# High weights against both halves of the activations: one product of 512 columns where there were two of 256

## The chip, the core and the metric

The kernel runs on one core of a Trainium2 chip. A core has a matrix engine (PE; the loading of its weights is listed as PEld), a vector engine (DVE), a scalar engine (ACT), a general engine (POOL) and a queue engine that issues the transfers (SP). Each works through its own list of instructions in order and waits on semaphores of the others. The metric is device time of one execution: 2247.73 us before the change, the median of three runs (2246.83 to 2248.64).

## The reference, cut to what matters

Two transformer blocks over 256 tokens of width 2048. The first (sparse attention, pooling, a mixture of 32 experts) is computed by instructions that the change leaves alone. The second has two layers:

```python
def even_layer(h, ...):                                   # layer 0
    z = h @ w_in                                          # 2048 x 4352
    lru_x, lru_gate, q, k, v, swa_gate = split_cols(z, EVEN_SPLITS)
    y_a = rg_lru(causal_depthwise_conv(lru_x, ...), ...) * silu(lru_gate)
    y_b = sliding_window_gqa_sinks(q, k, v, sinks) * silu(swa_gate)
    return concatenate([y_a, y_b]) @ w_out                # 2048 x 2048
def odd_layer(h, ...):                                    # layer 1
    z = h @ w_in                                          # 2048 x 6464
    c_q, c_kv, k_rope, mla_gate, dq, dk, dv, diff_gate = split_cols(z, ODD_SPLITS)
    ...
    return concatenate([y_c, y_d]) @ w_out
for layer in (0, 1):
    x = x + layer(rmsnorm(x, gain))
return rmsnorm(x, final_gain)
```

## The kernel before, in words

**Split products.** Every float32 matrix of the dense products is split into two halves of a shorter type (fp32r): a high half h (a cast on ACT, `ACT.copy(h, t)` in `prep`) and a low half l (a subtraction on DVE, `tt(l, t, f32(h), OP.subtract)` in `low`). A product is then three: high weights times high activations, high weights times low activations, low weights times high activations, all added up in the same place in PSUM.

**Chunks and steps.** `dense` computes a chunk of n output columns. In the form "T" the weights (128 rows x 128 columns) are PE's stationary operand, and the 256 tokens of the activations move through, so a group of 128 output columns (an m-tile) fills half a PSUM bank of 512 columns. In the form "tok" it is the other way round: the activations of 128 tokens are stationary and 512 weight columns move. `weight_steps` cuts a chunk into steps. For n = 512 a step holds 2 of the 16 row tiles k, for n = 256 it holds 4. A step of the form T at n = 512 is 2 x 4 x 3 = 24 products of 256 columns; a step of the form tok is 12 products of 512 columns. Each step has a raw weight tile (one of two 1 MB places, each of which serves two steps; SP loads it in pieces of 512 KB), a tile of halves (one of four places) and the products.

**Order.** The program writes out its order itself. In `run_steps` (ahead = 3, lag = 1), round i issues the load and cast of step i + 3, then the subtraction of step i + 2, then the products of step i, then one `bg.tick()`: one piece of the background tasks (recurrence, attention, norms) and one piece of the chain of evictions. In what follows a *round* is that. A chunk's evictions come one a round after its last step (`one_by_one`), and for the first chunk of a layer not before the norm of the tokens is ready. `scaled` multiplies an m-tile out of PSUM by that norm on DVE (`y<-acc,vr`, `dv<-acc,vr`, `z<-acc,vr`); `Join` combines a gate (its Tanh on ACT) with what it gates.

**Places.** PSUM has four banks "acc" for dense products, so two chunks of two banks; three banks "tps" for attention and transposes, one "ada". The next chunk but one takes a chunk's banks over.

**Attention.** `attend` works in rounds as well. For head i the scores are made (PE, L818, L1711), the masked scores and their extreme are taken (DVE, L749), the exponentials (ACT, L753; L756 for the sink), the division (DVE, L771); PE transposes P two rounds (L781, sliding window) later, the result is copied (PT, in turns by ACT and DVE), and the product with the values follows (L810, L812, L1744 to L1746). The stretches of the trace: recurrence 1490 to 1600 us, sliding window 1618 to 1690, layer 1 from about 1760, latent attention 1932 to 2005, differential attention 2044 to 2110, output projection and end from 2136.

Of the kernel before, what the change touches and what calls it, by code (L numbers as in the profile page):

```python
# [4 lines left out]
F32 = mybir.dt.float32  # L5
# [137 lines left out]
def fused_kernel(tc, a, out):  # L143
# [30 lines left out]
    with top:  # L174
# [261 lines left out]
        class Wide:  # L436


            def __init__(self, pool):
                self.pool, self.x, self.r, self.ready = pool, ({}, {}), {}, False  # L440
# [4 lines left out]
            def halves(self, j):  # L445
                r = []
                for i in (0, 1):
                    n = 2 * (j // 4) + i
                    if n not in self.r:
                        self.r[n] = self.pool.tile([128, 4, 2, S], F32R, name=f"a{n}")  # L450
                    r.append(self.r[n][:, j % 4])
                    for k in (0, 1):
                        self.x[i][2 * j + k] = r[i][:, k]
                return r
# [44 lines left out]
        def weight_steps(w, KT, c0, n, mm, done, load=None, order=None, apart=0):  # L499


            steps, late = [], []
            cell = {}
            order = order or [(k0, min(4, KT - k0)) for k0 in range(0, KT, 4)]
            b = 4 if n <= 256 else 2
            ks = [(k0, kn, k) for k0, kn in order for k in range(k0, k0 + kn, b)]
            for i, (k0, kn, k) in enumerate(ks):

                def prep(k0=k0, k=k, kn=kn):
                    if k == k0:  # L510
                        cell["raw", k0] = t = raw()
                        if load:
                            load(t, k0, kn)
                        else:
                            for k1 in range(0, kn, pieces[0]):
                                kk = min(kn - k1, pieces[0])
                                SP.dma_start(t[:, k1:k1 + kk, 0:n],
                                             w[(k0 + k1) * 128:(k0 + k1 + kk) * 128, c0:c0 + n]
                                             .rearrange("(k p) n -> p k n", p=128))
                    t = cell["raw", k0][:, k - k0:k - k0 + b, 0:n]  # L520
                    x = half_places.next()
                    if b == 4:
                        x = x.rearrange("p k (i n) -> p (k i) n", i=2)
                    h, l = x[:, 0:b, 0:n], x[:, b:2 * b, 0:n]
                    cell[k] = (h, l, t)
                    ACT.copy(h, t)  # L526

                def low(k=k):
                    h, l, t = cell[k]
                    tt(l, t, f32(h), OP.subtract)  # L530

                def step(k=k, i=i, ts=(0, 1)):
                    for j in range(b):
                        mm(k + j, cell[k][0][:, j], cell[k][1][:, j], i + j == 0, i + 1 == len(ks) and j + 1 == b, ts)
                    if i + 1 == len(ks):
                        done(ts)
                if i < len(ks) - apart:
                    steps.append(Dense(prep, step, low))
                else:
                    steps.append(Dense(prep, (lambda f=step: f(ts=(0,))), low))  # L540
                    late.append(Dense(lambda: None, (lambda f=step: f(ts=(1,)))))
            return steps + late

        def dense(w, KT, c0, n, acts, outs, load=None, order=None, apart=0):


            regs, bank, off = [], -1, 512
            for kind, arg, m, ev in outs:
                for t in ((0,) if kind == "T" else (0, 1)):
                    wd = S if kind == "T" else m  # L550
                    if off + wd > 512:
                        bank, off = bank + 1, 0
                    regs.append((kind, arg, m, ev, t, bank, off, wd))
                    off += wd
# [6 lines left out]
            def mm(k, h, l, first, last, ts):  # L561
# [3 lines left out]
                for r in regs:  # L565
                    kind, arg, m, _, t, b, o, wd = r
                    if t not in ts:
                        continue
                    if kind == "T":
# [11 lines left out]
            def out(r, x):  # L581
                return (r[3](x) if r[0] == "T" else r[3](r[4], x)) or ()
# [18 lines left out]
            return weight_steps(w, KT, c0, n, mm, done, load, order, apart)  # L601

# [850 lines left out]
        ytile = lambda i, c, dt=F32R: yt.tile([128, S], dt, name=f"y{i}_{c}")  # L1453

        class Join:
# [16 lines left out]
            def join(self, c, slot, src, gate, scale):  # L1472
# [6 lines left out]
                h, l = (ytile(i, self.first + c) for i in (0, 1))  # L1479
# [3 lines left out]
                self.yT[0][self.first + c], self.yT[1][self.first + c] = h, l  # L1483
# [9 lines left out]
        hT, yT = norm.hT, [{}, {}]  # L1493
# [11 lines left out]
        lo_slot = lambda first: lambda c: ytile(1, first + c, F32)  # L1505
# [89 lines left out]
        steps += dense_T(wi0, KD, 512, 512, hT, to_xr)  # L1595
        steps[7].then = lambda: bg.add(lru(0))
        steps[15].then = lambda: bg.add(lru(1))
        for c0 in (2048, 2560):
            steps += dense_T(wi0, KD, c0, 512, hT, lambda c, p: norm.scaled(q0[:, c - 16], p))
        steps += dense(wi0, KD, 3072, 256, hT, [("T", 0, 128, k_ev), ("T", 128, 128, lambda p: norm.scaled(vT0, p))])  # L1600
        steps[-1].then = lambda: bg.add(swa())
        for c0 in (1024, 1536):
            steps += dense_T(wi0, KD, c0, 512, hT, lambda c, p: join_a(c - 8, p, True))
        for c0 in (3328, 3840):
            steps += dense_T(wi0, KD, c0, 512, hT, lambda c, p: join_b(c - 26, p, True))
# [4 lines left out]
        x, y, *z = [dense_T(wo0, KD, n0, 512, yT, add_xT)  # L1610
                    for n0 in range(0, D, 512)]
# [17 lines left out]
        def odd():  # L1629
            hT, yT = norm1.hT, [{}, {}]  # L1630
# [25 lines left out]
            def scratch(i, c):  # L1656
                if (i, c) not in held:
                    held[i, c] = ytile(i, c, F32)
                return held[i, c]
# [116 lines left out]
            steps = dense_T(wi1, KD, 0, 512, hT, to_c) + dense_T(wi1, KD, 512, 512, hT, to_c)  # L1776
# [3 lines left out]
            for c0 in (2368, 2880):  # L1780
                steps += dense(wi1, KD, c0, 512, hT, [("T", m * 128, 128, (lambda p, h=(c0 - 2368) // 128 + m: norm1.scaled(dqT(h), p)))
                                                      for m in range(4)])
# [33 lines left out]
            for c0 in (3392, 3904):  # L1816
                steps += dense(wi1, KD, c0, 512, hT, [("T", m * 128, 128, (lambda p, h=(c0 - 3392) // 128 + m: norm1.scaled(dkT(h), p)))
                                                      for m in range(4)])
# [8 lines left out]
            for c0 in (1344, 1856):  # L1827
                steps += dense(wi1, KD, c0, 512, hT, [("T", m * 128, 128, (lambda p, c=(c0 - 1344) // 128 + m: join_c(c, p, True)))
                                                      for m in range(4)])
            for c0 in (5440, 5952):  # L1830
                steps += dense(wi1, KD, c0, 512, hT, [("T", m * 128, 128, (lambda p, c=(c0 - 5440) // 128 + m: join_d(c, p, True)))
                                                      for m in range(4)])
# [71 lines left out]
```

## Time and profile before

| | |
|---|---|
| time, median of three runs | 2247.73 us |
| time of the profiled execution | 2247.3 us |
| its span | 2245.5 us |
| PE busy over the span | 1900.1 us (85%) |
| DVE, ACT busy over the span | 989.5 us (44%), 629.7 us (28%) |
| the second block's dense stretch, 1476 to 2231 us | PE busy 754.95 of 755 us |

Busy time is an average over stages of different kinds: the first 1400 us wait for transfers of expert weights, the rest is PE's. A wait in brackets behind a row is the time that its engine sat idle before that instruction, and whom it waited for. The ends of PE's rows are modelled, so PE is read from start to start.

### The profile page before, as it was taken

What the parts mean: (1) busy time and instruction counts of PE and PEld (TensorE: products, weight loads), DVE (VectorE), ACT (ScalarE), POOL (GpSimd) and SP (SyncE); (2) the same over time, 40 slices, a digit from 0 to 9 for tenths busy, and PEclk for the clock granted to TensorE, in tenths of its full rate; (3) what the DMA queues carried; (4) which work ended last, traced back from release to release, by engine and by line L of the source; (5) the groups of instructions that cost most, each with busy time, mean ns of one, the idle gap of its engine ahead of it and who ended that gap; (6) DMA issues with size and microseconds to landing.
All of it is one profiled execution on the core that took longest, in us unless ns stands there. A gap on an engine that the chain in (4) does not pass through costs nothing.

```text
span 2245.5 us, 35044 instructions
## 1 busy us (share of the span) xinstructions
PE 1900.1 (85%) x14718; PEld 1369.9 (61%) x14718; DVE 989.5 (44%) x1866; ACT 629.7 (28%) x1072; POOL 73.3 (3%) x90
## 2 busy tenths in 40 slices
PE   5999999986768676666767575999999999999998
PEld 3666656662424242423333242699989999989986
DVE  2456736541212122121212120667886657556864
ACT  2333324311000000000000010355664444435543
POOL 2000100000000000000000000000000001200000
PEclk8999999998898788898989898999999999999999
DMA  9999898889999999999999999855536556444554
GB/s 336 382 359 338 318 379 297 307 345 410 389 420 421 421 420 421 421 421 421 421 421 420 421 413 422 310 177 169 181 124 187 177 171 179 150 150 151 169 188 149
DMA packets 198066, 694.94 MB, mean 309 GB/s; under 512 B 20455, under 2 KB 44553, under 8 KB 140433
## 3 DMA queue, kind: packets, MB, share of 16 engines
q1 hardware_dynamic: 194608, 682.03, 79.9%
q0 software_dynamic: 2000, 6.89, 1.0%
q10 hardware_dynamic: 1296, 3.74, 0.4%
q8 instruction: 117, 1.92, 0.3%
q14 instruction: 45, 0.36, 0.0%
HBM read 690.49 MB, written 2.11 MB: 308 GB/s over the span
## 4 chain that ended last, share of the span: by engine, by line
PE 42%; DMA 27%; DVE 2%; ACT 1%; issue 1%; SPq 0%; POOLq 0%; POOL 0%; ACTq 0%; DVEq 0%
PE acc L578 31%; DMA w<-in_w_dram 14%; DMA a<-in_w_dram 8%; PE acc L1151 4%; DMA wx<-in_w_dram 3%; DMA h<-in_w_dram 2%; PE acc L1186 2%; DVE Og L167 1%; PE acc L1216 1%; PE acc L1378 1%; PE tps L818 1%; PE tps L781 1%; PE tps L1711 0%; PE ada L810 0%; PE tps L1560 0%
## 5 line engine op out<-in xcount | busy, mean ns | idle before, releaser
L578 PE MATMUL acc<-h,h 128*128 128x512 f32 (+1 forms) x1152 | 277.4, 390 | 13.2 <-DVE h L167 5.2
L1186 PE MATMUL acc<-w,Xg 128*32 128x256 f32 x2176 | 213.1, 447 | 71.7 <-DMA w<-in_w_dram 71.2
L578 PEld LDWEIGHTS acc<-h,h 128*128 128x128 f32 x1152 | 203.4, 191 | 92.5 <-issue 23.6
L167 DVE TENSOR_TENSOR s<-s,acc 64x256 f32<-64x256 f32 (+1 forms) x34 | 14.9, 438 | 431.4 <-ACT s L1193 427.0
L1186 PEld LDWEIGHTS acc<-w,Xg 128*32 128x32 f32 x2176 | 92.5, 124 | 171.1 <-DMA w<-in_w_dram 103.0
L1193 ACT ACTIVATE s<-acc 64x256 f32<-64x256 f32 x32 | 12.1, 377 | 620.1 <-PE acc L1186 620.1
L167 DVE TENSOR_TENSOR Og<-acc,gt 32x512 f32<-32x512 f32 x124 | 85.2, 687 | 212.9 <-PE acc L1216 211.3
L1186 PE MATMUL acc<-a,Xg 128*32 128x256 f32 x1312 | 131.1, 455 | 52.9 <-DMA a<-in_w_dram 43.2
L167 DVE TENSOR_TENSOR h<-w,h 128x1024 fp32r<-128x1024 f32 (+2 forms) x106 | 124.3, 1176 | 67.6 <-ACT h L526 66.4
L526 ACT CAST h<-w 128x1024 fp32r<-128x1024 f32 (+2 forms) x106 | 105.7, 1002 | 108.5 <-PE acc L578 51.4
L1186 PEld LDWEIGHTS acc<-a,Xg 128*32 128x32 f32 x1312 | 56.3, 126 | 112.3 <-DMA a<-in_w_dram 60.8
L578 PE MATMUL acc<-a,w 128*128 128x256 f32 x948 | 122.1, 285 | 0.1
L578 PE MATMUL acc<-a,wx 128*128 128x256 f32 x948 | 121.8, 285 | 0.2 <-DVE wx L167 0.2
L1151 PE MATMUL acc<-Ps,x 128*128 128x128 f32 x448 | 99.4, 395 | 25.4 <-DVE Ps L1139 25.4
L578 PE MATMUL acc<-a,h 128*128 128x256 f32 (+1 forms) x924 | 118.9, 285 | 0.4 <-DVE h L167 0.4
L1151 PEld LDWEIGHTS acc<-Ps,x 128*128 128x128 f32 x448 | 98.3, 311 | 34.1 <-issue 34.1
L578 PEld LDWEIGHTS acc<-a,wx 128*128 128x128 f32 x948 | 116.4, 191 | 2.5 <-issue 2.0
L578 PEld LDWEIGHTS acc<-a,w 128*128 128x128 f32 x948 | 116.6, 191 | 1.8 <-issue 0.7
L578 PEld LDWEIGHTS acc<-a,h 128*128 128x128 f32 (+1 forms) x924 | 113.5, 191 | 2.1 <-issue 1.3
L578 PE MATMUL acc<-a,gt 128*128 128x256 f32 (+1 forms) x876 | 112.3, 284 | 0.0
L578 PEld LDWEIGHTS acc<-a,gt 128*128 128x128 f32 (+1 forms) x876 | 107.6, 191 | 1.8 <-issue 1.7
L1216 PE MATMUL acc<-w,aT 128*32 128x512 f32 x528 | 76.1, 675 | 34.0 <-DMA w<-in_w_dram 27.9
(496 smaller groups left out, 2816.7 us busy)
## 6 DMA issues: line engine op xcount, KB each, us to landing
w<-in_w_dram SPq DMA_DIRECT2D x205, 1024.0 KB, 19.8
a<-in_w_dram SPq DMA_DIRECT2D x116, 1024.0 KB, 19.8
w<-in_l_w_in_dram SPq DMA_DIRECT2D x160, 512.0 KB, 4.6
w<-in_w_ada_dram SPq DMA_DIRECT2D x42, 1024.0 KB, 7.5
w<-in_l_w_out_dram SPq DMA_DIRECT2D x64, 512.0 KB, 4.7
wx<-in_w_dram SPq DMA_DIRECT2D x30, 1024.0 KB, 19.8
h<-in_w_dram SPq DMA_DIRECT2D x29, 1024.0 KB, 19.8
w<-in_w_ada_dram SPq DMA_DIRECT2D x30, 512.0 KB, 10.1
```

The lines of the kernel that those rows point to most:

```text
L167: (e or DVE).tensor_tensor(out=o, in0=x, in1=y, op=op)
L526: ACT.copy(h, t)
L578: PE.matmul(out_of(r), lt, rt, start=first and i == 0 and o == 0, stop=last and i == 2, skip_group_check=True)
L781: PE.transpose(p[:, b * 128:(b + 1) * 128], P[h][:, b * 128:(b + 1) * 128], ident)
L818: PE.matmul(p[:, r], q[:, t * 128:(t + 1) * 128], k[:, 0:128 * (t + 1)], start=True, stop=True)
L1151: PE.matmul(b[:, (k - k0) * 128:(k - k0 + 1) * 128], x1[:, t, k:D:16], flat(Ps)[:, t], start=t == 0, stop=t == 1)
L1186: PE.matmul(p1[32 * j:32 * j + 32, 0:256], Xg[:, k, 32 * el:32 * el + 32], w[:, k % 4, (j % 2) * 256:(j % 2) * 256 + 256], start=k == 0, s ...
L1193: ACT.activation(s[0:64], p1[0:64, 0:256], AF.Silu)
L1216: PE.matmul(p2[32 * j:32 * j + 32, :], aT[:, kk % 2, (kk // 2) * 32:(kk // 2) * 32 + 32], down[kk][:, j * 512:(j + 1) * 512], start=kk == ...
L1378: PE.matmul(p, PWT[:, t * 128:(t + 1) * 128], Og[:, n:n + 512], start=True, stop=True)
```

## The change

A new form `dense_2T` replaces `dense_T` for 19 of the 512-column pieces of the second block: all but the first of layer 0's input projection, the last two of its output projection, and all T pieces of layer 1's input projection of width 1024 (latents, queries, keys and gates). It cuts each into two chunks of 256 columns. The two halves of the activations now lie side by side in one tile, and a product with the high weights moves both, 512 columns, into a whole bank; the product with the low weights moves the high half alone, 256 columns, into the bank's first half. At eviction ACT copies the bank's second half to SBUF, DVE adds the first half to it, and the old eviction goes on from the sum.

```diff
+            narrow = n == 256 and KT == KD and not order
+            kt = 8 if narrow else 4
...
+                            part = pieces[0] * kt // 4
+                            for k1 in range(0, kn, part):
+                                kk = min(kn - k1, part)
...
+            both = 2 if apart is None else 1
+            apart = apart or 0
...
-                    wd = S if kind == "T" else m
+                    wd = (S * both if kind == "T" else m)
...
+                    if kind == "T" and both == 2:
+                        PE.matmul(out_of(r).rearrange("p (i s) -> p i s", i=2), h[:, arg:arg + m], acts[2][k],
+                                  start=first, stop=False, skip_group_check=True)
+                        PE.matmul(out_of(r)[:, 0:S], l[:, arg:arg + m], acts[0][k], start=False, stop=last,
+                                  skip_group_check=True)
...
             def out(r, x):
+                if both == 2:
+                    side[0] ^= 1
+                    y = summed[0:x.shape[0], side[0]]
+                    ACT.copy(y, x[:, S:2 * S])
+                    tt(y, y, x[:, 0:S], OP.add)
+                    x = y
...
+        def dense_2T(w, KT, c0, n, acts, ev):
+            r = []
+            for c in range(c0, c0 + n, 256):
+                r += dense(w, KT, c, 256, acts, [("T", m, 128, (lambda p, c=(c + m) // 128: ev(c, p))) for m in (0, 128)], apart=None)
+            return r
...
+        summed = pp.tile([128, 2, S], F32, name="sel")
```

A raw tile of 1 MB now holds 8 row tiles of 256 columns in place of 4 of 512, in rows of 1 KB in place of 2 KB, still two steps' worth and still in pieces of 512 KB.

The first place where the order changes is on PE, early in layer 0. There the first chunk (banks acc_8653 and acc_8654) is still of 512 columns, and the norm becomes ready in round 10. PE at the end of step 11 and the start of step 12 in the kernel before (a0 to a3: activations; wx_8972, h_9009: the halves of the weights of the steps 11 and 12):

```order
L578 MATMUL acc_8976<-a1_8567,wx_8972 128x256
L578 MATMUL acc_8976<-a0_8566,wx_8972 128x256
L578 MATMUL acc_8975<-a2_8703,h_9009 128x256 [waits Activation_49]
L578 MATMUL acc_8975<-a3_8704,h_9009 128x256
L578 MATMUL acc_8975<-a2_8703,h_9009 128x256 x2
L578 MATMUL acc_8975<-a3_8704,h_9009 128x256
L578 MATMUL acc_8975<-a2_8703,h_9009 128x256
```

PE at the end of step 11 and the start of step 12 in the changed kernel (here a0 and a3 are tiles that hold both halves of the activations):

```order
L576 MATMUL acc_8977<-a3_8718,wx_8973 128x512
L578 MATMUL acc_8977<-a3_8718,wx_8973 128x256
L576 MATMUL acc_9075<-a0_8566,h_9002 128x512 [waits DVE_49,Activation_49]
L578 MATMUL acc_9075<-a0_8566,h_9002 128x256
L576 MATMUL acc_9076<-a0_8566,h_9002 128x512 [waits DVE_49]
```

Before, step 12 goes on in the banks of the second chunk. Now step 12 opens a third chunk, which takes over the two banks of the first, each after a wait for DVE. The count that the second of these waits for stands at the fourth of the evictions shown next.

DVE at the same place in the changed kernel, rounds 10 to 13 (dv<-acc: evictions of the first chunk; 128x1024 rows: the low halves of the steps 13 to 15); the kernel before has the same rows here, under other buffer numbers:

```order
L1339 TENSOR_SCALAR PT<-K,rs 128x128 x2
L167 TENSOR_TENSOR dv<-acc,vr 128x256
L167 TENSOR_TENSOR gt_9021<-w_8999,gt_9021 128x1024
L167 TENSOR_TENSOR dv<-acc,vr 128x256
L167 TENSOR_TENSOR w_9052<-w_9049,w_9052 128x1024
L167 TENSOR_TENSOR dv<-acc,vr 128x256
L167 TENSOR_TENSOR wx<-w_9049,wx 128x1024
L167 TENSOR_TENSOR dv<-acc,vr 128x256
```

Nothing moved in this list: what is new is that PE's step 12 waits for its last row, which stands behind the low half of step 15.

The second place is a round of the sliding window attention in which an m-tile of a gate is evicted. DVE before (P, st: scores and sums of a head; y_10931: the gate's m-tile):

```order
L749 ISA P_10916,st_10923<-tps_10917,masks_8736,sink_3575 128x256
L749 ISA st_10923 128x1
L167 TENSOR_TENSOR y_10931<-acc_10455,vr_9069 128x256
L167 TENSOR_TENSOR gt2_10869<-w0_10816,gt2_10869 128x1024
L167 TENSOR_TENSOR y1_8_10908<-y_10905,y0_8_10907 128x256
L164 SCALAR_TENSOR_TENSOR y1_11_10930<-y1_11_10930,y_10931 128x256
```

DVE in the changed kernel:

```order
L777 ISA P_10509,st_10516<-tps_10510,masks_8737,sink_3575 128x256
L777 ISA st_10516 128x1
L167 TENSOR_TENSOR sel_8730<-sel_8730,acc_10307 128x256
L167 TENSOR_TENSOR y_10526<-sel_8730,vr_9046 128x256
L167 TENSOR_TENSOR wx_10469<-w1_10423,wx_10469 128x1024
L167 TENSOR_TENSOR y8_10501<-y_10499,y8_10501 128x256
L164 SCALAR_TENSOR_TENSOR y11_10525<-y11_10525,y_10526 128x256
```

ACT in the same round of the changed kernel:

```order
L781 ACTIVATE P_10509,st_10516<-P_10509,st_10516 128x128
L781 ACTIVATE P_10509,st_10516<-P_10509,st_10516 128x256
L784 ACTIVATE st_10516<-sink_3575,st_10516 128x1 x2
L597 COPY sel_8730<-acc_10307 128x256
L1519 ACTIVATE y11_10525<-y_10526 128x256
L530 CAST h_10532<-w0_10529 128x1024
```

DVE's eviction now begins with a sum that reads what ACT's COPY wrote, and that COPY stands behind the four exponentials of the head in the same round.

## Rows read from the trace of the kernel before

**Rows 1.** Windows: us, busy PE, PEld, DVE, ACT, POOL, PEclk, DMA share, GB/s.

```profile
1476.00:2231.00 755.00, 754.95 (x5693) 712.08 (x5692) 506.39 (x919) 382.62 (x645) 35.76 (x33) 1.00 0.53 165
1618.00:1690.00 72.00, 72.00 (x602) 64.90 (x601) 59.04 (x184) 47.56 (x137) 0.00 (x0) 1.00 0.39 127
1938.00:1985.00 47.00, 47.00 (x337) 41.73 (x336) 21.84 (x55) 16.61 (x35) 0.00 (x0) 1.00 0.37 117
2044.00:2110.00 66.00, 66.00 (x554) 62.42 (x554) 57.54 (x177) 39.51 (x105) 0.00 (x0) 1.00 0.41 129
```

**Rows 2.** Chain of waits from 1690 to 1940 us: start, us, what.

```profile
1774.09 74.54 PE acc L578 x624
```

**Rows 3.** Timeline of PE at a tok chunk's end: start, us, engine, line, what.

```profile
2032.55 2.88 PE L578 MATMUL acc<-h,a 128*128 128x512 f32 x12
2035.27 3.04 PE L578 MATMUL acc<-a,gt 128*128 128x256 f32 x24
...
2041.02 3.04 PE L578 MATMUL acc<-a,wx 128*128 128x256 f32 x24
```

**Rows 4.** Timeline of PE in the two latent up-projections.

```profile
1875.19 2.99 PE L578 MATMUL acc<-z,gt 128*128 128x256 f32 x24
1878.02 2.99 PE L578 MATMUL acc<-z,w 128*128 128x256 f32 x24
...
1898.52 0.88 PE L578 MATMUL acc<-gt,dv 128*128 128x256 f32 x6
1899.24 0.88 PE L578 MATMUL acc<-dv,gt 128*128 128x256 f32 x6
```

**Rows 5.** Timeline of PE, steps 11 to 13 of layer 0.

```profile
1476.20 3.11 PE L578 MATMUL acc<-a,wx 128*128 128x256 f32 x24
1479.15 3.04 PE L578 MATMUL acc<-a,h 128*128 128x256 f32 x24
1482.03 3.04 PE L578 MATMUL acc<-a,gt 128*128 128x256 f32 x24
```

**Rows 6.** Timeline of DVE in the same stretch.

```profile
1480.43 1.23 DVE L167 TENSOR_TENSOR wx<-w,wx 128x1024 fp32r<-128x1024 f32 x1 [0.18 <-ACT wx L526]
1481.57 0.42 DVE L167 TENSOR_TENSOR dv<-acc,vr 128x256 f32<-128x256 f32 x1
```

**Rows 7.** Timeline of all engines in the sliding window attention.

```profile
1618.92 0.37 ACT L153 COPY P<-tps 128x256 f32<-128x256 f32 x1 [2.01 <-PE tps L1525]
...
1638.17 0.35 DVE L749 CUSTOM_DVE_ANT_0 P<-tps,masks,sink 128x128 f32<-128x128 f32 x1 [0.29 <-PE tps L818]
1638.45 0.48 DVE L749 CUSTOM_DVE_ANT_0 P<-tps,masks,sink 128x256 f32<-128x256 f32 x1
1638.86 0.42 DVE L167 TENSOR_TENSOR y<-acc,vr 128x256 f32<-128x256 f32 x1
1639.48 0.47 ACT L756 ACTIVATE st<-sink,st 128x1 f32<-128x1 f32 x2
1641.38 0.55 DVE L771 TENSOR_SCALAR P<-P,st 128x128 f32<-128x128 f32 x2
1645.14 0.55 PE L781 MATMUL tps<-K,P 128*128 128x128 f32 x3
1645.26 0.42 DVE L164 SCALAR_TENSOR_TENSOR y<-ada,y 128x256 f32<-128x256 f32 x1 [0.66 <-PE ada L812]
```

**Rows 8.** Timeline: a step's cast, low half and products.

```profile
1595.10 1.05 ACT L526 CAST h<-w 128x1024 fp32r<-128x1024 f32 x1 [1.40 <-DMA w<-in_l_w_in_dram]
1597.11 1.22 DVE L167 TENSOR_TENSOR h<-w,h 128x1024 fp32r<-128x1024 f32 x1
1601.23 3.04 PE L578 MATMUL acc<-a,h 128*128 128x256 f32 x24
```

**Rows 9.** DMA queues, 1690 to 1770, then 1795 to 1812 us: packets, MB, share.

```profile
q1 hardware_dynamic: 7081, 13.65, 54.0%
q1 hardware_dynamic: 1674, 2.02, 40.2%
```

More of the change, by code (lines that the diff above doesn't have):

```diff
@@ L445, in halves @@
             def halves(self, j):
[L446 to L454, printed above, removed]
+                n = j // 2
+                if n not in self.r:
+                    self.r[n] = self.pool.tile([128, 2, 2, 2, S], F32R, name=f"a{n}")
+                t = self.r[n][:, j % 2]
+                for k in (0, 1):
+                    self.x[0][2 * j + k], self.x[1][2 * j + k], self.x[2][2 * j + k] = t[:, 0, k], t[:, 1, k], t[:, :, k]
+                return [t[:, 0], t[:, 1]]
         class Acts:
@@ L503, in weight_steps @@
             cell = {}
-            order = order or [(k0, min(4, KT - k0)) for k0 in range(0, KT, 4)]
+            narrow = n == 256 and KT == KD and not order
+            kt = 8 if narrow else 4
+            order = order or [(k0, min(kt, KT - k0)) for k0 in range(0, KT, kt)]
             b = 4 if n <= 256 else 2
@@ L1478, in join @@
                     stt(y, src, scale, slot, OP.mult, OP.mult)
-                h, l = (ytile(i, self.first + c) for i in (0, 1))
+                hl = ytile(self.first + c)
+                h, l = hl[:, 0], hl[:, 1]
                 ACT.copy(h, y)
@@ L1482, in join @@
                 tt(l, y, f32(h), OP.subtract)
-                self.yT[0][self.first + c], self.yT[1][self.first + c] = h, l
+                for i, x in enumerate((h, l, hl)):
+                    self.yT[i][self.first + c] = x
             def twice_silu(self, o, g):
@@ L1598, in fused_kernel @@
         for c0 in (2048, 2560):
[L1599 removed]
+            steps += dense_2T(wi0, KD, c0, 512, hT, lambda c, p: norm.scaled(q0[:, c - 16], p))
         steps += dense(wi0, KD, 3072, 256, hT, [("T", 0, 128, k_ev), ("T", 128, 128, lambda p: norm.scaled(vT0, p))])
@@ L1609, in add_xT @@
                 bg.add(norm1.pair(c // 2))
-        x, y, *z = [dense_T(wo0, KD, n0, 512, yT, add_xT)
-                    for n0 in range(0, D, 512)]
+        x, y, *z = [f(wo0, KD, n0, 512, yT, add_xT)
+                    for n0, f in zip(range(0, D, 512), (dense_T, dense_T, dense_2T, dense_2T))]
         y[3].then = lambda: (bg.drain(), odd())
@@ L1779, in odd @@
             steps[-1].then = lambda: bg.add(latents())
-            for c0 in (2368, 2880):
-                steps += dense(wi1, KD, c0, 512, hT, [("T", m * 128, 128, (lambda p, h=(c0 - 2368) // 128 + m: norm1.scaled(dqT(h), p)))
-                                                      for m in range(4)])
+            steps += dense_2T(wi1, KD, 2368, 1024, hT, lambda c, p: norm1.scaled(dqT(c - 18), p))
             def up_ready():
@@ L1815, in odd @@
             join_c, join_d = Join(slot("c"), yT, 0, norm1), Join(slot("d"), yT, 8, norm1)
-            for c0 in (3392, 3904):
-                steps += dense(wi1, KD, c0, 512, hT, [("T", m * 128, 128, (lambda p, h=(c0 - 3392) // 128 + m: norm1.scaled(dkT(h), p)))
-                                                      for m in range(4)])
+            steps += dense_2T(wi1, KD, 3392, 1024, hT, lambda c, p: norm1.scaled(dkT(c - 26), p))
             def new_dv():
@@ L1826, in odd @@
             steps[-1].then = lambda: bg.add(diff())
[L1827 to L1832, printed above, removed]
+            steps += dense_2T(wi1, KD, 1344, 1024, hT, lambda c, p: join_c(c - 10, p, True))
+            steps += dense_2T(wi1, KD, 5440, 1024, hT, lambda c, p: join_d(c - 42, p, True))
             steps[-1].then = bg.finish
```

33 lines of the change are left out of this document (18 added, 15 removed).

## The prediction, made before the changed kernel was run

> **What bounds the kernel now.** I read the windows first. Over the whole dense stretch of the second block, 1476 to 2231 us, PE is busy 754.95 of 755 us at a granted clock of 1.00, DVE 506, ACT 383, the transfers a share of 0.53 [rows 1]. The chain of waits says the same: one piece of 624 products after the other, with nothing of another engine between them [rows 2]. So a microsecond taken off PE's work here is a microsecond of the end, as long as no other engine becomes late. I therefore looked next at what one product costs PE, from start to start, and then at DVE, which is the nearest to being late: in the sliding window attention it is busy 59.0 of 72 us, in the differential attention 57.5 of 66, in the latent attention only 21.8 of 47 [rows 1].
>
> **The products.** The change moves the same columns with fewer instructions. Of three products per row tile and m-tile two are left, 512 and 256 columns in place of three of 256. It touches 19 pieces of 512 columns, so 38 chunks of 4 steps, 152 steps of 24 products (6144 columns) that become 152 of 16. What does a product cost beyond its columns? A tok step moves 6144 columns too, in 12 products: 2035.27 - 2032.55 = 2.72 us. A T step takes them in 24: (2041.02 - 2035.27) / 2 = 2.875 us [rows 3]. The 12 products more cost 0.155 us, 12.9 ns each, and 2.72 - 12 x 0.0129 = 2.565 us is left for the columns, which is 2.4 GHz. A new step is then 2.565 + 16 x 0.0129 = 2.77 us, 0.103 less, and 152 of them save 15.7 us. The bounds: the up-projections' T steps take 1878.02 - 1875.19 = 2.83 us [rows 4], by which a product costs 9.2 ns and the change saves 11.1; early layer 0 has 1482.03 - 1479.15 = 2.88 [rows 5], 13.3 ns and 16.2. The activations now move as two runs of 256. Six products that move weights in separated runs (acc<-gt,dv) take 1899.24 - 1898.52 = 0.72 us [rows 4], 120 ns each like any other, so I charge nothing for that.
>
> One rule of the Trainium skill speaks against this size. "TensorE: Matmul & The Clock Gate", section "Back-to-back issue gap", gives N / 2.4 + 2.5 ns between products, so that one product less is worth 2.5 ns. By that figure the 1216 products would be worth an estimated 3.0 us in place of 15.7. The trace's own gap is wider, 2.875 us / 24 = 119.8 ns for 256 columns [rows 3], and I go by it.
>
> **The evictions.** Each of the 76 m-tiles gets an ACT copy from PSUM (0.37 us [rows 7], a copy of the same size) and a DVE sum (0.42, as the product out of PSUM at 1638.86 [rows 7]). That is 28 us of ACT and 32 us of DVE in a stretch where they have 372 and 249 us free [rows 1], hidden under PE in all. The price lies in the order. DVE's sum waits for ACT's copy, and DVE is in order: behind the sum stand the low half of a coming step and the division of the head's P. In a round of softmax the copy stands behind the four exponentials. DVE's masked scores end at 1638.93, ACT's last exponential at 1639.95 [rows 7]; the copy ends 0.37 later. DVE idles some 1.4 us where it now goes straight on, and with the sum (0.35 in the pipeline) it is 1.75 us later. By the order 15 evictions share a round with a softmax: 7 in the sliding window, 4 in the latent, 4 in the differential attention.
>
> Sliding window: 7 x 1.75 = 12.25 us of lag. It meets two covers. The first is DVE's waits for PE, 0.66 + 0.29 us in two rounds [rows 7]; the seven lie in 12 rounds, which give back 5.7, less the 12 x 0.103 = 1.3 by which PE itself comes sooner, 4.4 us. The second is how early P is ready: divided by 1641.93, transposed by PE at 1645.14 [rows 7], 3.2 us. What is left, 12.25 - 4.4 - 3.2 = 4.7 us, reaches PE. The bounds are 0 (the lows are made two steps ahead and the attention is not what PE waits for) and 12.3 (no cover). I take 4.7. Differential: 4 x 1.75 = 7 us against 66 - 57.5 = 8.5 us of DVE's idle time [rows 1]; latent: 7 us against 25. For both together and the last rounds of the recurrence I put 0.5 us, between 0 and 7.
>
> **The banks.** A chunk is now half as long and still takes two banks, so the next but one comes sooner. This matters in one place. The norm of layer 0 is ready in round 10 and the first chunk's four evictions go out in rounds 10 to 13, while step 12 already opens the third chunk in the same banks. Its second bank waits for the fourth eviction. On DVE that one stands behind the low half of step 15, this behind the cast of step 15 on ACT, and this needs the halves' place that PE frees at the end of step 11. Before, step 11 ended at 1479.15 and the fourth eviction at 1481.57 + 0.42 = 1481.99 [rows 5, 6]; PE has the first m-tile of the row tile (0.35 us) to do until then. PE will stand for 1481.99 - 1479.15 - 0.35 = 2.5 us. It is at most 2.8 (the cast 1.05 and the low half 1.22 [rows 8], the eviction 0.42, handoffs 0.1) and at least 0. All later chunks take banks whose evictions are a round old or more, and behind no later low half than PE needs anyway.
>
> **The transfers.** Pieces of 512 KB come in rows of 1 KB in place of 2. A packet of 1.93 KB takes 0.540 x 80 x 16 / 7081 = 97.6 ns, one of 1.21 KB (the chunk of 320 columns) 0.402 x 17 x 16 / 1674 = 65.3 ns [rows 9], 51 and 54 ns per KB, so at 1 KB some 56, a tenth slower. A piece lands half a us later. A cast that waited 1.40 us for its transfer still had its low half done at 1598.3, 2.9 us ahead of the products at 1601.23 [rows 8]. That hides it: nothing. Without that cover it would be half a us per pair of steps, up to 38 us, but neither the transfers nor SP come near their limit at a share of 0.53.
>
> **The sum.** 2247.3 (profiled execution) - 15.7 (products) + 2.5 (banks) + 4.7 (sliding window) + 0.5 (other rounds) = 2239.3 us. The median lies 0.4 above the profiled execution, so 2239.7 us.
>
> **Rivals.** The first: the lag is covered. DVE's work on P and the low halves is all a round or two ahead, and PE is busy through all 72 us of that attention [rows 1]. Then it is 2247.7 - 15.7 + 2.5 = 2234.5. Against it: DVE's chain is nearly closed there, its waits for PE being under 1 us in 8.4.
>
> The second, slower: the copy behind the exponentials holds DVE, and the lag passes to PE at its full price, because P, its transposes and the next scores are a ring that has to go round. All 15 at 1.75 us are 26 us: 2247.7 - 15.7 + 2.5 + 26 = 2260.5. It decides from the eleventh of the 15 on: 10 x 1.75 + 2.5 leaves 4.3 us over what is saved. For it speaks how full DVE is in two of the three stretches, against it the latent one.
>
> The third: a product does not get cheaper. The 12.9 ns would then belong to the tok form (activations stationary), and a pair of 512 and 256 would cost what the three did. Then only the prices remain: 2247.7 + 2.5 + 4.7 + 0.5 = 2255.4. Both forms load a full 128 x 128 tile for each product, and columns at exactly 2.4 GHz speak against it. By the Trainium skill's figure above this would be an estimated 2252.4.
>
> **How the numbers follow.** A measurement of this kernel tells 0.2%, 4.5 us, from no change, so faster is below 2243.2 and slower above 2252.2. I give the forecast (2235.5 to 2243) 0.55, the covered lag 0.15, so faster 0.70. That half or more of the lag of all three attentions reaches PE and the time ends in between has 0.21. The full price has 0.05 and the third rival 0.04, slower 0.09. The range goes from the largest saving with one stall (2247.7 - 16.2 + 0.5) = 2232 to 2249, beyond which lie the slower rivals; the likeliest case's own is 2235 to 2244.
>
> **What would show it.** Right: 16 products in 2.77 us in the undisturbed stretches; at the start of the third chunk a wait of PE for DVE of 2 to 3 us, once; in the sliding window rounds with an eviction a DVE sum that waits over a us for ACT, and P's transposes waiting for DVE by some 5 us in all, none to speak of in the latent attention. Wrong: 16 products in 2.87 us (third rival), waits of PE for DVE in all three attentions (second), or for transfers (the rows of 1 KB). Everything before 1440 us should stand as it was.

## The result, and the profile after

The changed kernel takes 2261.9 us (median of 7 runs, 2258.4 to 2264.67) against 2249.36 us before (7 runs), a ratio of 1.0055 with a 95% interval of 1.0046 to 1.0065. It is slower, by 0.55%; the prediction was 2239.7 us and faster. The profiled span is 2257.9 us, 12.4 more than before. The second block begins at the same place (its first dense product at 1442.5 us, before 1442.0) and takes 805.8 us from its first product to its last, before 794.0. So 11.8 us of the 12.4 lie there.

The windows of the changed kernel, in the columns of [rows 1]; the first row answers to the first one there:

```profile
1476.00:2243.00 767.00, 753.92 (x4500) 651.58 (x4499) 535.89 (x993) 402.23 (x719) 35.94 (x33) 0.99 0.53 163
...
1572.00:1588.00 16.00, 14.14 (x73) 12.07 (x72) 13.34 (x21) 10.81 (x15) 0.00 (x0) 0.89 0.37 117
...
1620.00:1636.00 16.00, 14.49 (x79) 11.58 (x78) 11.75 (x35) 10.58 (x28) 0.00 (x0) 0.89 0.45 137
2100.00:2116.00 16.00, 11.14 (x71) 9.27 (x70) 14.26 (x47) 10.10 (x28) 0.00 (x0) 1.00 0.40 118
2116.00:2132.00 16.00, 16.00 (x89) 14.15 (x89) 10.73 (x16) 7.90 (x12) 1.97 (x1) 0.89 0.42 130
```

Two things are new. PE stands idle for 13 us, where before it was busy for 754.95 of 755 us. And in three stretches the granted clock is 0.89 over 16 us, that is, about 3.4 us at the lower of the two levels; everywhere else from 1460 to 2244 us it is 1.00. The rate there can be read from two successive pairs of products in the first of these stretches:

```profile
1580.74 0.63 PE L576 MATMUL acc<-a,wx 128*128 128x512 f32 x1
...
1581.38 0.63 PE L576 MATMUL acc<-a,wx 128*128 128x512 f32 x1
```

A pair takes 0.64 us there and 0.35 us at full clock, so by an estimate from these rows PE loses nearly 1.6 us each time, 4.7 us in all.

PE's waits from 1400 us on (waiting line, what it waits for, us in total, times, longest):

```profile
PE ada L1775 <- DVE PT L155: 5.5, 2, 4.9
PE acc L1244 <- DMA w<-in_w_dram: 3.5, 3, 2.9
PE acc L576 <- DVE dv L167: 2.4, 1, 2.4
PE acc L578 <- DVE wx L167: 2.3, 2, 1.9
PE tps L809 <- DVE P L799: 1.5, 1, 1.5
```

Only the second row is older (the first block's end). The first is the differential attention (PT), the third the bank at layer 0's third chunk, the fourth a low half beside the recurrence's last work, the fifth the sliding window's P. All four wait for DVE. The wait for the bank is this one:

```profile
1482.29 0.51 PE L576 MATMUL acc<-a,h 128*128 128x512 f32 x1 [2.37 <-DVE dv L167]
```

It stands ahead of the first sum. In the other three DVE is late, and DVE's sums wait for ACT. The view by tile of the sums (engine, operation, count, ns minimum/median/maximum), and what DVE stood idle for ahead of them (us, times):

```profile
L597 ACT COPY sel<-acc x76: 345/365/378, 1488.9 to 2163.6; 128x256 f32<-128x256 f32 x76
L167 DVE TENSOR_TENSOR sel<-sel,acc x76: 359/420/424, 1489.3 to 2164.0; 128x256 f32<-128x256 f32 x76
...
  ACT sel L597: 67.9, 40
```

The operations cost what was put down for them, 0.37 and 0.42 us. But 40 of the 76 sums held DVE up, not 15. The 15 that the prediction named are among them: seven in the sliding window wait 1.30 us each, four in the latent attention 0.97, four in the differential attention 1.39, together 18.5 us. The other 25 copies stand behind casts, table loads and wide activations, 49.4 us. Eight of these (24.2 us) lie between 1740 and 1860 us, where the steps lost almost nothing by it. The first that makes PE wait for more than half a us stands behind no softmax. Timeline at the recurrence's end (start, us, engine, line, what; in brackets the idle time before and whom it waited for):

```profile
1574.12 1.28 ACT L1604 ACT_TABLE_LOAD   x1
1575.41 1.06 ACT L1604 ACTIVATE z<-s 128x1024 f32<-128x1024 f32 x1
1576.37 0.35 ACT L597 COPY sel<-acc 128x256 f32<-128x256 f32 x1
...
1576.76 0.42 DVE L167 TENSOR_TENSOR sel<-sel,acc 128x256 f32<-128x256 f32 x1 [2.49 <-ACT sel L597]
1577.21 0.42 DVE L167 TENSOR_TENSOR y<-sel,vr 128x256 f32<-128x256 f32 x1
1577.56 1.22 DVE L167 TENSOR_TENSOR wx<-w,wx 128x1024 fp32r<-128x1024 f32 x1
```

The copy stands behind a table load and an activation of 1024 columns, the sum behind the copy, the low half `wx` behind the sum, and PE gets it at 1578.83 after 1.86 us of waiting. The half-clock stretch begins at 1580.

The differential attention, in one of its last rounds:

```profile
2109.32 0.49 ACT L781 ACTIVATE P<-P,st 128x256 f32<-128x256 f32 x1
2109.72 0.18 ACT L781 ACTIVATION_READ_ACCUMULATOR P<-P,st 128x1 f32 x1
2109.82 0.35 ACT L597 COPY sel<-acc 128x256 f32<-128x256 f32 x1
2110.20 0.42 DVE L167 TENSOR_TENSOR sel<-sel,acc 128x256 f32<-128x256 f32 x1 [1.38 <-ACT sel L597]
...
2115.04 0.55 DVE L155 COPY PT<-tps 128x384 f32<-128x384 f32 x1
2115.51 1.22 DVE L167 TENSOR_TENSOR gt<-w,gt 128x1024 fp32r<-128x1024 f32 x1
2115.74 0.52 PE L1775 MATMUL ada<-dv,PT 128*128 128x128 f32 x2 [4.86 <-DVE PT L155]
```

Here the copy does stand behind the exponentials, and 1.38 us is what the prediction reckoned for it. From 2110.20 to 2115.04 DVE is busy without a gap, and PT comes at the end of that. The 4.86 us were not made in this round alone. The same sum one turn of the attention (four dense steps) earlier:

```profile
2093.63 0.42 DVE L167 TENSOR_TENSOR sel<-sel,acc 128x256 f32<-128x256 f32 x1 [1.39 <-ACT sel L597]
```

So DVE goes round in 16.57 us. PE's turn is shorter. It can be read from the changed kernel without its sums (`no_sum`, below), where DVE still waits for PE's scores in each turn:

```profile
2076.51 0.29 DVE L773 CUSTOM_DVE_ANT_0 P<-tps,masks 128x128 f32<-128x128 f32 x1 [0.85 <-PE tps L842]
...
2091.85 0.29 DVE L773 CUSTOM_DVE_ANT_0 P<-tps,masks 128x128 f32<-128x128 f32 x1 [0.85 <-PE tps L842]
```

That is 15.34 us. In the kernel before, such waits took 6.4 us from 2050 to 2112 us:

```profile
DVE P L749 <- PE tps L818: 6.4, 5, 1.6
```

In the changed kernel none is left from 2056 to 2115 us. DVE had become the slower of the two, by 1.23 us a turn, which by estimate is 4.9 us over the four turns of this attention. PE's waits for PT there are 0.62 and 4.86 us.

The products, undisturbed, first in the last pieces of layer 0's output projection, then in layer 1's queries (eight pairs from the first row to the last, each time):

```profile
1732.61 0.40 PE L576 MATMUL acc<-y,w 128*128 128x512 f32 x1
1732.84 0.28 PE L578 MATMUL acc<-y,w 128*128 128x256 f32 x1
1732.96 0.40 PE L576 MATMUL acc<-y,w 128*128 128x512 f32 x1
...
1735.43 0.40 PE L576 MATMUL acc<-y,wx 128*128 128x512 f32 x1
```

```profile
1842.41 0.40 PE L576 MATMUL acc<-a,wx 128*128 128x512 f32 x1
...
1845.18 0.40 PE L576 MATMUL acc<-a,h 128*128 128x512 f32 x1
```

A step of 16 products takes 2.82 us in the first and 2.77 in the second, in place of 2.875 [rows 3]. Of the 57 new steps in which PE did nothing else and waited for nothing, 26 take 2.77 us, as predicted, and 31 take 2.81 to 2.83.

### The profile page after: what moved, and what is told of

It reads as the page before. It is cut to its first block, busy times and chain, and to the rows that moved or that the text cites. A ratio compares the mean times of both kernels' runs of the same rounds, so it can differ in the third digit from the quotient of the medians.

```text
span 2257.9 us, 32750 instructions
## 1 busy us (share of the span) xinstructions
PE 1895.3 (84%) x13502; PEld 1306.2 (58%) x13502; DVE 1019.6 (45%) x1941; ACT 649.0 (29%) x1146; POOL 73.4 (3%) x90
## 4 chain that ended last, share of the span: by engine, by line
PE 32%; DMA 29%; DVE 9%; ACT 2%; issue 1%; SPq 0%; ACTq 0%; POOLq 0%; POOL 0%; DVEq 0%
DMA w<-in_w_dram 14%; PE acc L590 10%; DMA a<-in_w_dram 9%; PE acc L576 8%; PE acc L578 4%; PE acc L1179 4%; DMA wx<-in_w_dram 3%; DMA h<-in_w_dram 2%; PE acc L1214 2%; DMA w<-in_l_w_in_dram 1%; DVE y L167 1%; DVE w L167 1%; DVE wx L167 1%; DVE Og L167 1%; DVE P L777 1%
## 5 line engine op out<-in xcount | busy, mean ns | idle before, releaser
L576 PE MATMUL acc<-a,h 128*128 128x512 f32 x272 | 100.3, 407 | 2.8 <-DVE dv L167 2.4
L576 PE MATMUL acc<-a,wx 128*128 128x512 f32 x272 | 101.0, 410 | 0.0
L576 PE MATMUL acc<-a,gt 128*128 128x512 f32 x272 | 98.4, 402 | 0.0
L576 PE MATMUL acc<-a,w 128*128 128x512 f32 x272 | 98.3, 402 | 0.0
L167 DVE TENSOR_TENSOR wx<-w,wx 128x1024 fp32r<-128x1024 f32 (+1 forms) x64 | 78.0, 1218 | 19.0 <-ACT wx L530 18.8
L530 ACT CAST w<-w 128x1024 fp32r<-128x1024 f32 (+1 forms) x64 | 66.4, 1038 | 66.6 <-DMA w<-in_l_w_in_dram 28.8
L167 DVE TENSOR_TENSOR gt<-w,gt 128x1024 fp32r<-128x1024 f32 (+1 forms) x61 | 75.0, 1230 | 20.6 <-ACT gt L530 20.6
L157 ACT ACTIVATE Xg<-acc,shsc,g 128x128 f32<-128x128 f32 x64 | 29.3, 457 | 189.8 <-DVE Xg L161 107.7
```

Source lines behind the costliest of these rows:

```text
L157: ACT.activation(o, i, AF.Identity, bias=0.0 if bias is None else bias, scale=scale)
L167: (e or DVE).tensor_tensor(out=o, in0=x, in1=y, op=op)
L576: PE.matmul(out_of(r).rearrange("p (i s) -> p i s", i=2), h[:, arg:arg + m], acts[2][k], start=first, stop=False, skip_group_check=True)
```

## The experiments

Each was timed beside the kernel before. Every view is of one execution, and the first block alone moves by some 5 us between executions; so beside each time stands a table of the second block alone, worked out from the trace: the start of each dense step of PE, counted from the block's first product, compared with the same step of the kernel before. There are 264 steps. Steps 0 to 24 are layer 0's first three pieces, 24 to 32 its fourth; 32 to 80 hold the gates of join_a and join_b, beside the recurrence's end and the sliding window, and plain pieces behind them; 80 to 216 the rest of layer 0's output and of layer 1 (the gates of join_c last); 216 to 232 the gates of join_d. Gain (-) or loss (+) in us within each stretch:

| kernel | 0-24 | 24-32 | 32-80 | 80-216 | 216-232 | second block |
|---|---|---|---|---|---|---|
| changed | +2.3 | -0.9 | +8.2 | -3.8 | +5.9 | +11.8 |
| no_sum | +2.1 | -0.9 | -2.5 | -5.4 | -0.8 | -7.4 |
| three | +0.2 | 0.0 | -0.7 | 0.0 | 0.0 | -0.5 |
| grouped | +3.1 | -0.7 | +8.4 | -4.9 | +5.6 | +11.5 |
| reduce | +4.4 | -0.9 | -1.3 | -3.7 | +3.0 | +1.6 |
| sum_attention | 0.0 | 0.0 | +8.1 | +0.1 | -0.8 | +7.3 |
| sum_calm | +1.3 | -0.9 | 0.0 | -4.2 | +6.4 | +2.6 |
| mix | +1.4 | -0.4 | 0.0 | -3.1 | +3.6 | +1.4 |
| mix_grouped | +2.9 | -0.7 | 0.0 | -3.6 | +3.8 | +2.4 |
| away_alt | +0.3 | 0.0 | 0.0 | -4.0 | 0.0 | -3.7 |
| away | +0.4 | 0.0 | +0.2 | -3.6 | 0.0 | -3.1 |
| best | 0.0 | 0.0 | +1.2 | -3.9 | -0.8 | -3.5 |

### The sum taken away

```diff
-                    side[0] ^= 1
-                    y = summed[0:x.shape[0], side[0]]
-                    ACT.copy(y, x[:, S:2 * S])
-                    tt(y, y, x[:, 0:S], OP.add)
-                    x = y
+                    x = x[:, 0:S]
```

> The evictions of the 76 summed m-tiles read only the first half of their bank; ACT's copy and DVE's sum are gone, so the product of the high weights with the low activations is computed and left out of the output. All products, chunks and transfers stay as in the changed kernel. Theory W (the sums make PE wait, and the waits bring stretches of granted clock 0.50): of the 12.8 us of PE waits that the changed kernel has more than the one before from 1400 us on, only the 2.4 us at layer 0's third chunk, whose evictions have no sum, stay; the three stretches of 3.4 us at half clock go too (5.1 us); the cheaper products leave 7 us: 2249.4 - 7 + 2.4 + about 1 = 2246, between 2244 and 2248. Rival N (narrow chunks with 1 KB rows make PE wait): the waits stay, 2257 or more.

2240.91 us, ratio 0.9969 (0.9958 to 0.9981). PE's waits from 1440 us on:

```profile
PE acc L576 <- DVE dv L167: 2.9, 2, 2.4
PE acc L578 <- DVE h L167: 0.4, 1, 0.4
PE acc L590 <- DVE wx L167: 0.4, 1, 0.4
PE tps L1444 <- DVE gt L167: 0.2, 1, 0.2
```

The waits for P, PT and low halves are gone and with them all stretches at half clock. The bank wait of 2.4 us stays. Copy and sum cost the changed kernel 19.2 us of its second block: 4.1 in the steps 32 to 52 (the recurrence's end), 6.5 in 52 to 72 (the sliding window), 7.6 in the differential attention, 0.9 elsewhere. The second block came 4 us below what was expected (-7.4 for -3.6): a step was taken to gain 46 ns, but an undisturbed one gains 53 or 107 ns. The column 24-32 is of the second kind, 0.85 us in eight steps. Without the bank wait the products give -7.4 - 2.4 = -9.8 us.

### Narrow chunks alone

```diff
-            both = 2 if apart is None else 1
+            both = 1
```

> The chunks of 256 columns with 1 KB rows stay, but each row tile of an m-tile takes three products of 256 columns again, and the evictions have no sum. Theory W: nothing is won on the products, and of the waits only the 2.4 us at the third chunk stay: 2249.4 + 2.4 = 2251.8, between 2250 and 2253.5. Rival N (narrow chunks): PE waits of 1 us and more at many chunk ends and stretches at half clock, 2256 or more.

2247.56 us, ratio 0.9993 (0.9984 to 1.0002), no change. No wait over 0.4 us is left; the bank wait is gone too, which was not expected: both m-tiles of a chunk then share one bank. The chunks of 256 columns and the transfers in rows of 1 KB cost nothing. Between this kernel and the one without sums lie 6.9 us of the second block, or 9.3 without the latter's bank wait of 2.4: by the two runs the wide product is worth 9.3 to 9.8 us, 61 to 65 ns a step in the mean.

### The order of the products

Products of 512 columns of all row tiles first, then those of 256:

```diff
+                    for p in getattr(mm, "parts", (None,)):
                         for j in range(b):
-                        mm(k + j, ...)
+                            mm(k + j, ..., p)
...
+                        if p == 0:
                             PE.matmul(..., h[:, arg:arg + m], acts[2][k], ...)
+                        else:
                             PE.matmul(..., l[:, arg:arg + m], acts[0][k], ...)
```

> In a step all eight products of 512 columns stand first and then all eight of 256, in place of 512, 256, 512, 256. In the changed kernel a pair takes 353.5 ns (233 + 117 between starts); the 512-column products of the tok form take 226.7 ns one behind the other, those of 256 columns 119.9. Theory S (a change of width from one product to the next costs the 7 ns): a step falls from 2.83 to about 2.78 us, 152 steps give 7.5 us, and the low half has 1.8 us more before it is needed, so that the 1.9 us wait for a low half and its stretch at half clock (1.7 us) go: about 2251. Rival P (the pair has this price in any order): steps stay at 2.83 us; only the wait for the low half may go, 2258 to 2262.

2263.76 us, ratio 1.0056 (1.0043 to 1.0069). The steps did get shorter:

```profile
1731.64 2.00 PE L579 MATMUL acc<-y,h 128*128 128x512 f32 x8
1733.48 1.12 PE L582 MATMUL acc<-y,h 128*128 128x256 f32 x8
1734.43 2.00 PE L579 MATMUL acc<-y,gt 128*128 128x512 f32 x8
```

2.79 us a step, 0.03 below the slower of the two rates above. But the alternating order reaches 2.77 elsewhere, so a change of width does not by itself cost the 7 ns of theory S. An undisturbed step gains 88 ns grouped, and 53 or 107 alternating. In the joins PE now waits longer (P 3.3 us in place of 1.5), and this kernel too has three stretches at half clock, one of them behind the bank wait. So the time says nothing for or against the order; the stretch 80 to 216 does, with 1.1 us more gained.

### No wait for ACT

```diff
-                    ACT.copy(y, x[:, S:2 * S])
-                    tt(y, y, x[:, 0:S], OP.add)
+                    DVE.tensor_reduce(out=y, in_=x.rearrange("p (i s) -> p s i", i=2), axis=AX.X, op=OP.add)
```

> ACT's copy and DVE's sum are replaced by one DVE reduction over the bank's two halves (512 values read, 256 written), so no eviction waits for ACT. DVE is busy for about 0.7 us in it (it takes 0.69 us for 512 values a partition in the trace), 0.28 us more than for the sum. Theory W1 (DVE standing still behind ACT's copy, up to 2.5 us each, is what reaches PE): the 1.9 us wait for a low half, the 1.5 us wait for P and most of the 4.9 us wait for PT go, with their stretches at half clock: 2249 to 2254. Rival D (the time that DVE itself is busy for the sum is what reaches PE): the waits stay or grow, 2261 or more.

2249.48 us, ratio 0.9997 (0.9988 to 1.0006). DVE is busy 17 us more than in the changed kernel (page: 1036.8 against 1019.6), and yet 10.2 of the 11.8 us are gone:

```profile
L597 DVE TENSOR_REDUCE sel<-acc x76: 628/684/692, 1492.5 to 2154.3; 128x256 f32<-128x512 f32 x76
```

```profile
PE acc L576 <- DVE dv L167: 2.4, 1, 2.4
PE ada L1774 <- DVE PT L155: 2.1, 1, 2.1
PE acc L590 <- DVE w L167: 1.1, 1, 1.1
PE acc L578 <- DVE wx L167: 0.9, 1, 0.9
```

Beside the kernel without sums this shows where the standing still counted. In the sliding window (steps 52 to 72) copy and sum cost 6.5 us and the reduction nothing (-0.2); at the recurrence's end it is 4.1 against 1.3. There it was DVE's standing still behind ACT, not its work, that reached PE. In the differential attention 3.9 of the 7.6 us stay: from 2053 to 2109 us DVE never stands still and needs 15.65 us a turn against PE's 15.34, so its work counts there too. The 0-24 column holds the bank wait with a stretch at half clock behind it. One reserve: the reduction also takes 28 us of copies off ACT, and that ACT's later work gained by it was not tested apart; by its waits PE stood for ACT itself only 0.7 us in the changed kernel.

### Where the loss is made

Only the gates of join_a, join_b and join_d by the wide product; then the complement (the gates of join_a, join_b and join_d and layer 0's second piece by `dense_T`, the rest wide). Of the complement's edit one line:

```diff
-            steps += dense_2T(wi0, KD, c0, 512, hT, lambda c, p: join_a(c - 8, p, True))
+            steps += dense_T(wi0, KD, c0, 512, hT, lambda c, p: join_a(c - 8, p, True))
```

> The wide product, ACT's copy and DVE's sum only in the six pieces that run beside the recurrence's end, the sliding-window and the differential attention (the gates of join_a, join_b and join_d, 48 of the 152 steps); the other pieces are as in the kernel before. Theory W (the whole loss is made there): 48 steps give 48 x 0.045 = 2.2 us; the waits of 1.9, 1.5, 0.4 and 5.5 us and the three stretches of 3.4 us at half clock (5.1 us) come: 2249.5 - 2.2 + 14.4 = 2261.7, between 2257 and 2264. Rival (the lag of DVE builds up over all pieces): the waits are shorter, 2253 or less.

> The complement: the wide product with copy and sum in 12 pieces (96 steps), the gates of join_a, join_b and join_d and layer 0's second piece by three products of 256 columns. Theory W: no wait for P, PT or a low half, no stretch at half clock after 1420 us; 96 x 0.045 = 4.3 us are won, a bank wait of up to 2.4 us may come at the next two-bank piece: 2249.5 - 4.3 + 0 to 2.4 = 2245 to 2248. Rival (lag over all pieces): waits at other places of 3 us or more in sum, 2250 or more.

2256.18 us, ratio 1.0035 (1.0021 to 1.0049), and 2253.96 us, ratio 1.0025 (1.0015 to 1.0036). Neither is what was expected; the waits say why, first of the three gates, then of the complement:

```profile
PE acc L578 <- DVE wx L167: 3.7, 3, 1.4
PE acc L578 <- DVE w L167: 1.3, 1, 1.3
PE ada L838 <- ACT PT L153: 0.7, 2, 0.4
```

```profile
PE ada L1775 <- DVE PT L155: 5.3, 2, 4.7
PE acc L576 <- DVE dv L167: 1.6, 1, 1.6
```

The loss of join_a and join_b is all there (+8.1), here without a stretch at half clock: the low halves are waited for longer in its place. The wait for PT is with the complement: a chunk's evictions come a round each behind its last step, so what is evicted in the differential attention are the gates of join_c. Those of join_d come after it and cost nothing (-0.8).

### Mixed forms

The complement again with the reduction, alternating and grouped (edits as above):

> The calm pieces as in the run before it here, with the reduction by DVE alone in place of copy and sum. Theory W: where no exponentials stand before the copy, the copy costs PE nothing, so that both kernels take the same time within 1.5 us: 2244 to 2248. Rival D (DVE's busy time counts): this one is slower by 1 us and more, by the 48 x 0.28 = 13 us that DVE works longer, as far as they reach PE.

> The same, with all products of 512 columns of a step ahead of those of 256. With both orders in all 152 steps a step took 2.797 us grouped and 2.828 us alternating; that it did not show in the time there is put down to waits (P 3.3 us, PT 5.8 us) and stretches at half clock that the attentions brought. If that is so, 96 x 0.031 = 3.0 us are won on the alternating one: 2241 to 2245. If the grouped order has a price of its own, no gain, 2246 or more.

2251.1 us, ratio 1.0004 (0.9995 to 1.0013), and 2248.5 us, ratio 0.9999 (0.999 to 1.0008). The calm pieces were not all calm: with the gates of join_c among them PE still waits 1.8 and 2.0 us for PT, each time with a stretch at half clock; the grouped one has another behind a bank wait of 1.8 us. The reduction has a price of its own where nothing holds the copy up (80 to 216: 1.1 us less gained than with copy and sum). On the grouped order the pair is inconclusive. The steps 22 to 31 take 2.83 us each in the alternating one, and 2.77 in the complement with copy and sum, whose products and their order are the same: the two rates do not come from the order of the products.

### The wide product kept away from the attentions

`dense_2T` only in eight pieces whose evictions meet no softmax (edits as above, join_c's gates now plain too):

> The wide product with copy and sum only in eight pieces (64 steps): the last two pieces of layer 0's output projection, and of layer 1 those at columns 0, 2368 and 3392; the gates of all four joins and the recurrence's inputs by three products of 256 columns. Theory W (in the run with 12 pieces the 4.7 us wait for PT and its stretch at half clock came from the gates of join_c, whose m-tiles are evicted in the differential attention's rounds, and 1.6 us from a bank at layer 0's third chunk): both go, nothing new comes. The second block, from its first product to the last, took 794.0 us in the kernel before and 796.5 with 12 pieces: 794.0 - 64 x 0.047 = 791.0; time 2249.1 - 3 = 2246. Rival (the wait belongs to the attention's own pace): 796 and a time of 2250 or more.

> The same eight pieces with a step's eight products of 512 columns ahead of its eight of 256. If grouping is worth 31 ns a step where no wait stands beside it (2.797 against 2.828 us): 64 x 0.031 = 2.0 us less than the alternating one, second block 789, time 2244. If what grouping wins comes back as waits, as in the two runs with the reduction (795.3 alternating, 796.4 grouped): 791 or more, 2246 or more.

2245.91 us, ratio 0.9985 (0.9976 to 0.9994), and 2246.26 us, ratio 0.9983 (0.9973 to 0.9993). No PE wait over 0.4 us in the first, no stretch at half clock before the end. The grouped form gains more where the alternating steps run at their slower rate (0.7 us in eight, against 0.43), less where they run at the faster (0.68 against 0.84), and loses 1.0 us to low halves near the latent's up-projection; it is not worth more here.

The last kernel adds the gates of join_d (copy and sum) and of join_a and join_b (reduction):

```diff
+                    if by_sum:
+                        DVE.tensor_reduce(out=y, in_=x.rearrange("p (i s) -> p s i", i=2), axis=AX.X, op=OP.add)
+                    else:
                         ACT.copy(y, x[:, S:2 * S])
                         tt(y, y, x[:, 0:S], OP.add)
```

> 14 pieces (112 steps) with the wide product: the eight of the run with 64 steps by copy and sum, the gates of join_d by copy and sum too, the gates of join_a and join_b, which are evicted beside the exponentials of the sliding-window attention, by the reduction on DVE alone. By the starts of every eighth step, the stretch of join_a and join_b lost 8.2 us with copy and sum in the changed kernel and won 1.3 us with the reduction; that of join_d won 0.8 us where join_c was plain; the eight pieces won 3.7 us. Theory W: second block 794.0 - 3.7 - 1.3 - 0.8 = 788.2, time 2248.9 - 5.8 = 2243, between 2241.5 and 2245. Rival (the joins' pieces still bring a bank wait or a stretch at half clock): 2246 or more.

2246.12 us, ratio 0.998 (0.9971 to 0.9989). join_d gave its 0.8 us, join_a and join_b cost 1.2: PE waits 3.2 us for low halves there. These three kernels beat both the kernel before and the changed one, by some 3 to 4 us on the former, and can't be told apart.

## Why the prediction was wrong

**What bounds the kernel** held: PE did. Before, it had no idle time there, and 11.8 of the 12.4 us were lost between its first dense product of the second block and its last.

**The products: the mechanism held, the size did not.** "152 of them save 15.7 us" took every new step at 2.77 us. In 26 of 57 undisturbed steps that is what a step takes, 346.6 ns a pair as reckoned; in the other 31 a pair takes some 353 ns. By the runs without the sum and with narrow chunks alone the products are worth 9.3 to 9.8 us, below the lower bound of 11.1. What sets the rate of a step is open; the order of the products does not, as the steps 22 to 31 show. The estimate from the Trainium skill ("TensorE: Matmul & The Clock Gate", "Back-to-back issue gap"), 3.0 us, is too low for this kernel as well. The page gives that formula for a product by itself and says that in a stream the weight loads set the spacing too, which the prediction left out.

**The banks** were right: 2.37 us at 1482.29, predicted 2.5, and it stays without the sums and with the reduction.

**The evictions: the step that failed and turned the sign.** "For both together and the last rounds of the recurrence I put 0.5 us". Measured against the kernel without sums, copy and sum cost 7.6 us in the differential attention and 4.1 at the recurrence's end, 11.7 in all; each holds one stretch at half clock, by estimate 1.6 us.

- Differential attention: the count (4) and the lag (1.38 us) were right. But eight m-tiles are evicted there and each has a sum, of which the prediction charged four. Set against that was DVE's idle time of 8.5 us, as if it were free cover. It was used up: of DVE's waits for PE nothing is left, DVE's turn is 16.57 us against PE's 15.34, and the rest passed to PE. The latent attention cost nothing, as said: the steps beside it take the same time with the sums and without.
- The recurrence's end: the prediction looked for the copy behind exponentials alone. The copy that cost PE most there stood behind a table load and an activation of 1024 columns.
- Sliding window: 6.5 us, of which by estimate 1.6 are the clock, in place of 4.7. This term was near. Without sums DVE waits 5.7 us there for PE ahead of its masked scores, in the changed kernel 0.8; so the cover that the prediction named was there, and was spent.

**The clock** was not in the sum at all. The three stretches at half clock cost by estimate 4.7 us of the above; without the sums there is none.

**The transfers** cost nothing, as said.

By these sizes: -9.8 (products) + 2.4 (bank) + 4.1 (recurrence's end) + 6.5 (sliding window) + 7.6 (differential attention) + 0.9 (elsewhere) = +11.7 of the 11.8 measured. This splits the difference between runs and does not prove each part: PE's idle time (13.1 us) and the clock (4.7) less the products give 8 us. The rest lies in steps that take longer while the page shows PE busy; it was not traced.

The second rival named the mechanism, DVE held by ACT's copy with its lag passed on to PE. That its time, 2260.5, came near is luck: it had the products at 15.7 us for 9.8 and the lag at 26 for 19.2, left out the clock and the recurrence, and charged the latent attention, which cost nothing.

## What to carry to other kernels

An eviction that gains a step on another engine makes that engine's whole queue a part of the eviction: count what stands ahead of the new step in each round, not only its duration, and prefer a longer operation on one engine (0.68 us) to two short ones on two (0.37 + 0.42) where either queue is full. Apply a cheaper product only to the pieces whose evictions meet no other work; here 64 of 152 steps gained as much (3.7 us) as 112 did (3.5). And where one engine's turn is nearly as long as that of the engine that bounds, compare the two turns with all new work in them (here 16.57 us against 15.34): idle time covers a lag only until it is used up.

## What the runs showed of the hardware

A short wait of PE can cost more than itself. In the changed kernel waits of 1.86, 1.51 and 4.86 us were each followed, within 2 us, by some 3.4 us at half clock; one of 2.37 us at 1482 us was not, though the same wait was in the run with the reduction (PEclk, the third column from the right, first the changed kernel, then that run):

```profile
1476.00:1492.00 16.00, 13.63 (x79) 11.65 (x78) 8.12 (x11) 6.02 (x8) 0.00 (x0) 1.00 0.48 149
```

```profile
1480.00:1496.00 16.00, 13.63 (x71) 11.62 (x71) 8.39 (x11) 4.63 (x6) 0.00 (x0) 0.89 0.45 143
```

What decides between the two was not settled. Waits of up to 1.4 us in the run with three gates alone were followed by none.

The same 16 products take 2.77 or 2.83 us a step, with nothing else on PE and at the same granted clock. What decides that was not settled either.

DVE's reduction is called its slowest operation by the Trainium skill ("VectorE: DVE Perf Modes", "Rules for kernel authors"). Here 512 values a partition out of PSUM took 0.68 us, less than the copy and the sum that it replaced.
